# Streamed operands of a hybrid decoder trunk at the lower end of SBUF, weights and constants at the upper end

## The chip, the cores and the metric

The kernel runs on one core of one Trainium2 chip. The metric is the device time of one execution in microseconds (us). Beside timed runs there is one execution taken by the hardware profiler; it has a time of its own.

## What is computed

The reference is a trunk of two layers on a sequence of 1,024 positions with 1,024 features in float32. Cut to what matters:

```python
for layer in range(2):
    hn = rms_norm(h, norm_mix_g[layer])
    if layer % 2 == 0:   # gated DeltaNet heads and short convolutions
        h = h + mixer_ab(hn, ab_w_in[i], ..., ab_w_out[i])
    else:                # HGRN2 heads and dilated window attention
        h = h + mixer_cd(hn, cd_w_in[i], ..., cd_w_out[i])
    hn = rms_norm(h, norm_ffn_g[layer])
    h = h + (silu(hn @ ffn_w_gate[layer]) * (hn @ ffn_w_up[layer])) @ ffn_w_down[layer]
return rms_norm(h, norm_final_g)
```

The hidden size of the FFN is 2,816, or 22 blocks of 128. Nearly all the work is matrix products: the mixers' input and output projections, and the three products of each FFN.

## The kernel before, in words

Features lie on the 128 partitions, positions along the free dimension, in two halves of 512 positions. A float32 number is kept as a pair of fp32r numbers, high and low (`split`, lines 100 to 103: ScalarE makes the high part, VectorE or GpSimd the rest), and a product of two such pairs is three matmuls, written by `mm3` at lines 126, 127 and 128: high by high, high by low, low by high. Each streams 512 columns of an activation operand past a stationary 128 x 128 block of weights. `v_rows` (lines 989 to 999) is the exception: there the activations are stationary and the weights are streamed, 256 columns at a time.

The stages are, in order: mixer_ab (layer 0), its output projection, the FFN's gate and up stage (class Up), the FFN's down stage (`down`), and the same with mixer_cd for layer 1.

**Up** computes gate and up of a block f of 128 hidden units for both halves of the sequence with seven half-size products instead of eight, from sums and differences of operands and weights. Its streamed operands are b11, b21 (names hn in the profile), t1 and b22, and t2, t3 and t4. Per block f there are seven products (p1, p2, p5, p6, p7 and the two in `end`), each 4 x 3 = 12 matmuls. The first three blocks are ordered by hand (`turn`, under a manual schedule); the rest is ordered by the scheduler of the language, by priorities and its own estimate of times.

**down** multiplies hidden activations, read back from DRAM into the tile hr and split into a tile hidq, by the down weights. One hidq tile holds two blocks f (high, low, high, low). The line

```python
p, b = (hx, 6) if n[0] % 14 < 6 else (hnp, 8)
```

(512) puts the n-th hidq tile into the pool hx or into the pool hnp. Each of the 8 output blocks d streams all 22 blocks f.

**Memory.** A pool is a stretch of SBUF that grows from the left (low addresses) or the right (high addresses), in the order in which pools are opened; a closed pool's bytes are used again, and the new tile waits for the last use of the old ones on its bytes. Addresses are bytes within a partition. The low 16,512 bytes are taken by the run time, and usable memory ends at 229,344. Before the change the compiled program has these places:

| pool | what it holds | side | bytes |
|---|---|---|---|
| ring | weights: 4 split units `w` (8 KiB each), 2 raw buffers (4 KiB) | left | 16,512 to 57,472 |
| hnp | 8 slots of 8 KiB: hn, b11, b21, t1, b22, hidq | left | 57,472 to 123,008 |
| const | constants (cf, ci, vec, ones and so on) | left | 123,008 to 127,968 |
| sums (in Up) | a spare raw buffer and the sums of weights `ws` | left | 128,000 to 136,192 |
| hx (in Up) | 6 slots of 8 KiB: high and low parts of t2, t3, t4 | left | 136,192 to 185,344 |
| hx (in down) | 6 slots of 8 KiB: hidq | left | 127,968 to 177,120 |
| hr (in down) | 4 buffers of 2 KiB: hidden activations from DRAM | left | 177,120 to 185,312 |
| up (in Up) | 2 more weight units `w`, hid, u2, c22 | right | 196,480 to 229,248 |

The mixers' own pools lie behind const on the left and at the upper end on the right. Small tiles named "pad" (96 bytes in Trunk.begin, lines 163 and 164, and in Up.run, line 399; 32 bytes in Up.turn, line 403) shift what lies behind them.

All transfers are issued on SyncE's queue (`dma`, line 56), in the order that the scheduler gives them. The pools are opened at lines 66 to 70 and, for Up, at lines 1469 and 1470; `down` gets its pools at lines 1477 to 1479.

Of the kernel before, what the change touches and what calls it, by code (L numbers as in the profile page):

```python
# [9 lines left out]
F32 = mybir.dt.float32  # L10
# [8 lines left out]
P = 128  # L19
# [33 lines left out]
def hybrid_trunk_kernel(ctx: ExitStack, tc: tile.TileContext, x_t, w_all, w_down, w_ba, vecs, c_f, c_i, c_rope, out):  # L53
# [4 lines left out]
    def pool(name, side="left", space=None):  # L58
        kw = {} if space is None else {"space": space}
        if space is None:  # L60
            kw["side"] = side
        if space is not DRAM:
            kw["reuse_waits"] = "tile"
        return tc.tile_pool(name=name, bufs=1, **kw)

    ring = ctx.enter_context(pool("ring"))
    hnp = ctx.enter_context(pool("hnp"))
    const = ctx.enter_context(pool("const"))
    ps = ctx.enter_context(pool("ps", space=PSUM))
    dr = ctx.enter_context(pool("dr", space=DRAM))  # L70


    cf = const.tile([P, C_RM], F32, name="cf")
# [11 lines left out]
    onesn = const.tile([P, 1], F32, name="onesn")  # L85
    V.memset(onesn, 1.0 / DM)
    mhalf = const.tile([P, 16], F32, name="mhalf")
    V.memset(mhalf, -0.5)

    def psg():  # L90
        return ps.tile([P, HT], F32, tag="g", name="psg", bufs=2)
# [4 lines left out]
    def psm():  # L96
        return ps.tile([P, HT], F32, tag="m", name="psm", bufs=3)


    def split(hi, lo, src, eng=V):  # L100

        S.copy(hi, src)  # L102
        eng.tensor_tensor(lo, src, hi.bitcast(F32), op=SUB)  # L103

    def unit():

        return ring.tile([P, 2, DM], F32R, tag="w", name="w", bufs=4)

    def wload(*names):

        us = []
        for n in names:
            us.append(unit())
            raw = ring.tile([P, DM], F32, tag="raw", name="raw", bufs=2)
            dma(raw, w_all[W_AT[n]])
            split(us[-1][:, 0, :], us[-1][:, 1, :], raw)
        return us
# [21 lines left out]
    def quarter(pool_=None, name="hn"):  # L139

        p, n = (hnp, 8) if pool_ is None else (pool_, 6)
        return tuple(p.tile([P, KH, HT], F32R, tag="hn", name=name + "hl"[z], bufs=n) for z in range(2))
# [5 lines left out]
    class Trunk:  # L148
# [10 lines left out]
        def begin(self, half, src):  # L159

            self.h[half] = [self.hp.tile([P, KH, HT], F32, tag=f"h{half}{i}", name=f"h{half}{i}", bufs=1)
                            for i in range(2)]
            if half == 1:
                self.hp.tile([P, 24], F32, name="pad")
            for d in range(KT):
                dma(self.at(half, d), src[:, d, :])

# [78 lines left out]
    class Up:  # L246
# [133 lines left out]
        def run(self, tr, row, b11, b21, hx, close, left, right):  # L380

            E = mybir.EngineType
            with tc.manual_schedule(engines={E.PE, E.DVE, E.Activation, E.Pool}):
                b22, t3, t4 = self.turn(tr, row, b11, b21, hx, close, left, right)
            t1, t2 = self.t12
            self.weights(3)
            self.p7(2, t3)
            for f in range(3, NF):
                if f > 3:
                    self.weights(f)  # L390
                self.p1(f, b11)
                self.p2(f, b21, psm())
                self.end(f - 1, t4, b22)
                self.c11(f)
                self.p6(f, t2)
                self.p5(f, t1, psg())
                self.p7(f, t3)
            self.end(NF - 1, t4, b22)
            self.right.tile([P, 24], F32, name="pad")

        def turn(self, tr, row, b11, b21, hx, close, left, right):

            self.left.tile([P, 8], F32, name="pad")
            for f in range(2):
                self.part_a(f, self.raw("g", f))
            u0 = self.raw("u", 0, True)
            self.part_a(2, self.raw("g", 2))
            g0 = self.raw("g", 0)
            s = self.sums(g0, u0)
            G.tensor_tensor(u0[:, :HT], g0[:, :HT], u0[:, :HT], op=SUB)  # L410
            G.tensor_tensor(g0[:, HT:], g0[:, HT:], s[:, :HT], op=SUB)
            low = self.prepared(0, s, "s2", "s1")
            self.p1(0, b11)
            dg = tr.rms(1, between=low)
            self.p2(0, b21, psg())
            pb = tr.spread(dg)
            self.p1(1, b11)
            self.p2(1, b21, psg())
            self.p1(2, b11)
            self.p2(2, b21, psm())  # L420
            tr.short.close()
            self.snaps = left("snaps")

            (a0, b0), (a1, b1) = tr.h[0], tr.h[1]
            lo, hi = slice(0, 2), slice(2, 4)
            t1, b22 = quarter(name="t1"), quarter(name="b22")
            t2, t3, t4 = quarter(hx, "t2"), quarter(hx, "t3"), quarter(hx, "t4")
            self.t12 = t1, t2

            def comb(dst, x, y, c):  # L430
                V.tensor_tensor(dst[:, c, :], x[:, c, :], y[:, c, :], op=SUB)

            def high(t, src):
                for c in (lo, hi):
                    S.copy(t[0][:, c, :], src[:, c, :])

            def rest(t, src):
                for c in (lo, hi):
                    V.tensor_tensor(t[1][:, c, :], src[:, c, :], t[0][:, c, :].bitcast(F32), op=SUB)

            tr.scale(1, row, pb, (0,))
            self.part(0, u0, "s3", "a22")
            g1 = self.snap(0)
            u1 = self.raw("u", 1)
            tr.scale(1, row, pb, (1, 2, 3))
            comb(a0, a1, a0, lo)
            comb(a0, a1, a0, hi)
            high(t1, a0)
            s = self.left.tile([P, DM], F32, tag="s", name="ws", bufs=1)
            G.tensor_tensor(s[:, HT:], u1[:, :HT], u1[:, HT:], op=ADD)  # L450
            w1 = self.raw("g", 1, True)
            tr.scale(1, row, pb, range(KH, KT))
            rest(t1, a0)
            low_d = self.prepared(0, g0, None, "s4")
            self.p5(0, t1, psm())
            V.tensor_tensor(s[:, :HT], s[:, HT:], w1[:, :HT], op=SUB)
            low = self.prepared(1, s, "s2", "s1")
            comb(a0, b1, a0, lo)
            low()
            self.p5(1, t1, psm())  # L460
            comb(a0, b1, a0, hi)
            high(t2, a0)
            rest(t2, a0)
            g2 = self.snap(1)
            comb(a1, b1, a1, lo)
            comb(a1, b1, a1, hi)
            high(t3, a1)
            self.p6(0, t2)
            self.p6(1, t2)
            self.add11(0, g1)  # L470
            self.add11(1, g2)
            rest(t3, a1)
            V.tensor_tensor(u1[:, :HT], w1[:, :HT], u1[:, :HT], op=SUB)
            low = self.prepared(1, u1, "s3", "a22")
            comb(b0, b0, a0, lo)
            low()
            comb(b0, b0, a0, hi)
            high(t4, b0)
            low_d()
            u2 = self.raw("u", 2)  # L480
            rest(t4, b0)
            high(b22, b1)
            V.tensor_tensor(w1[:, HT:], w1[:, HT:], s[:, :HT], op=SUB)
            rest(b22, b1)
            close()
            self.right = right("up")
            self.part(1, w1, None, "s4")
            self.first = [self.hidden()]
            w2 = self.raw("g", 2)
            self.loads = 1  # L490
            s = self.sums(w2, u2)
            self.p7(0, t3)
            self.p7(1, t3)
            self.part_b(2, s)
            self.end(0, t4, b22)
            self.end(1, t4, b22)
            self.c11(2)
            self.p5(2, t1, psg())
            self.p6(2, t2)
            self.part_c(2, w2, u2)  # L500
            self.part_d(2, w2, s)
            return b22, t3, t4
# [920 lines left out]
    dma(cf[:, 0:P], c_f[:, 0:P])  # L1423
    dma(vec, vecs)
    first = [wload(("ab", 0), ("ab", 4)), wload(("ab", 8), ("ab", 12))]
    tr.begin(1, x_t[1])
    dma(cf[:, P:], c_f[:, P:C_RM])
    dma(ci, c_i)
# [15 lines left out]
    for layer in range(2):  # L1444
# [21 lines left out]


        with ExitStack() as fes:
            up = Up(layer, fes.enter_context(pool("sums")))
            hx = fes.enter_context(pool("hx"))  # L1470
            up.run(tr, row, *b1, hx, es.close, lambda n: fes.enter_context(pool(n)),
                   lambda n: fes.enter_context(pool(n, side="right")))

# [2 lines left out]
        with ExitStack() as fes:  # L1476
            hx = fes.enter_context(pool("hx"))
# [98 lines left out]
```

## Time and profile before

| | us |
|---|---|
| median of 3 runs | 2832.07 |
| lowest and highest run | 2829.3, 2838.61 |
| the profiled execution, its own time | 2837.84 |
| its span, first to last instruction | 2836.1 |

The mean granted clock of TensorE in the profiled execution is 0.987 of full speed.

How to read the rows: a line such as "L126 PE MATMUL psu<-t4h,w 128*128 128x512 f32" is one matmul of source line 126 that streams the tile t4h past weights w into the PSUM tile psu, 512 columns long. In the timeline the first column is the start in us from the span's start, the second the duration. Matmuls overlap, so the pace of TensorE is the difference of starts and not the duration. In the groups, "x176 | 69.3, 394 | 0.0" is the count, the busy us, the mean ns of one, and the idle us ahead of them with what ended it. PE is TensorE's matmuls, PEld its weight loads, DVE VectorE, ACT ScalarE, POOL GpSimd, SPq SyncE's queue of transfers.

### The profile page before, as it was taken

What the parts mean: (1) busy time and instruction counts of PE and PEld (TensorE: products, weight loads), DVE (VectorE), ACT (ScalarE), POOL (GpSimd) and SP (SyncE); (2) the same over time, 40 slices, a digit from 0 to 9 for tenths busy, and PEclk for the clock granted to TensorE, in tenths of its full rate; (3) what the DMA queues carried; (4) which work ended last, traced back from release to release, by engine and by line L of the source; (5) the groups of instructions that cost most, each with busy time, mean ns of one, the idle gap of its engine ahead of it and who ended that gap; (6) DMA issues with size and microseconds to landing.
All of it is one profiled execution on the core that took longest, in us unless ns stands there. A gap on an engine that the chain in (4) does not pass through costs nothing.

```text
span 2836.1 us, 37934 instructions
## 1 busy us (share of the span) xinstructions
PE 2730.9 (96%) x14974; PEld 2227.2 (79%) x14974; DVE 1502.4 (53%) x2599; ACT 1004.7 (35%) x1733; POOL 477.5 (17%) x435
## 2 busy tenths in 40 slices
PE   7999999989999989999999999999998999998998
PEld 5788877768787868889788897887876878876886
DVE  8766555573433343534765756666566334334342
ACT  5432122343333332323444434444434333333221
POOL 0110111333333201010000000000034333320000
PEclk9999999999999999999999999999999999999999
DMA  3334345522222274442132121323742222227442
GB/s 134 107 107 159 91 151 166 166 78 86 82 77 88 82 252 127 142 129 75 46 86 83 57 90 46 86 83 90 244 131 82 83 81 82 75 91 245 123 139 70
DMA packets 166178, 312.82 MB, mean 110 GB/s; under 512 B 22992, under 2 KB 70384, under 8 KB 164848
## 3 DMA queue, kind: packets, MB, share of 16 engines
q1 hardware_dynamic: 166000, 310.40, 34.8%
q8 instruction: 117, 1.92, 0.3%
q14 instruction: 61, 0.50, 0.1%
HBM read 236.32 MB, written 74.01 MB: 109 GB/s over the span
## 4 chain that ended last, share of the span: by engine, by line
PE 78%; DVE 8%; DMA 6%; ACT 4%; issue 3%; POOL 1%; SPq 0%; POOLq 0%; DVEq 0%; ACTq 0%
PE psu L126 17%; PE psu L128 16%; PE psu L127 16%; PE psm L128 4%; PE psm L127 4%; PE psm L126 4%; PE psg L128 3%; PE psg L127 3%; PE psg L126 3%; DMA hr<-hid 1%; DMA raw<-in_dram 1%; DVE w L103 1%; PE psm L1254 1%; DMA cxb<-scr_c 1%; DMA h<-hd 1%
## 5 line engine op out<-in xcount | busy, mean ns | idle before, releaser
L103 DVE TENSOR_TENSOR w<-raw,w 128x1024 fp32r<-128x1024 f32 (+1 forms) x336 | 408.6, 1218 | 610.2 <-ACT w L102 607.7
L102 ACT CAST w<-raw 128x1024 fp32r<-128x1024 f32 (+1 forms) x336 | 327.4, 975 | 649.6 <-PE psm L128 313.4
L126 PE MATMUL psu<-hnh,w 128*128 128x512 f32 x1328 | 532.0, 402 | 3.4 <-ACT w L102 1.9
L127 PE MATMUL psu<-hnl,w 128*128 128x512 f32 x1328 | 526.9, 397 | 0.5 <-DVE hnl L103 0.5
L128 PE MATMUL psu<-hnh,w 128*128 128x512 f32 x1328 | 524.8, 395 | 0.5 <-DVE w L103 0.5
L126 PEld LDWEIGHTS psu<-hnh,w 128*128 128x128 f32 x1328 | 250.7, 189 | 56.7 <-ACT hnh L102 3.5
L128 PEld LDWEIGHTS psu<-hnh,w 128*128 128x128 f32 x1328 | 250.9, 189 | 52.8 <-DVE w L103 1.6
L127 PEld LDWEIGHTS psu<-hnl,w 128*128 128x128 f32 x1328 | 250.7, 189 | 51.9 <-DVE hnl L103 1.9
L182 POOL TENSOR_TENSOR acc<-acc,sq 128x512 f32<-128x512 f32 x48 | 75.5, 1573 | 517.0 <-ACT sq L181 449.8
L126 PE MATMUL psm<-hidq,w 128*128 128x512 f32 x352 | 141.3, 401 | 19.0 <-ACT hidq L102 18.9
L126 PE MATMUL psu<-w,hnh 128*128 128x256 f32 x512 | 149.9, 293 | 0.0
L127 PE MATMUL psu<-w,hnh 128*128 128x256 f32 x512 | 145.3, 284 | 0.0
L128 PE MATMUL psu<-w,hnl 128*128 128x256 f32 x512 | 145.2, 284 | 0.0
L127 PE MATMUL psm<-hidq,w 128*128 128x512 f32 x352 | 141.5, 402 | 2.9 <-DVE hidq L103 2.9
L128 PE MATMUL psm<-hidq,w 128*128 128x512 f32 x352 | 140.1, 398 | 0.0
L126 PE MATMUL psu<-hidq,w 128*128 128x512 f32 x352 | 139.1, 395 | 0.0
L128 PE MATMUL psu<-hidq,w 128*128 128x512 f32 x352 | 138.6, 394 | 0.0
L127 PE MATMUL psu<-hidq,w 128*128 128x512 f32 x352 | 138.3, 393 | 0.0
L295 POOL TENSOR_TENSOR raw<-raw,ws 128x512 f32<-128x512 f32 x40 | 55.8, 1395 | 327.5 <-DVE w L103 327.5
L126 PEld LDWEIGHTS psu<-w,hnh 128*128 128x128 f32 x512 | 98.4, 192 | 0.8 <-issue 0.2
L127 PEld LDWEIGHTS psu<-w,hnh 128*128 128x128 f32 x512 | 98.4, 192 | 0.3 <-issue 0.2
L128 PEld LDWEIGHTS psu<-w,hnl 128*128 128x128 f32 x512 | 98.3, 192 | 0.0
(384 smaller groups left out, 5416.5 us busy)
## 6 DMA issues: line engine op xcount, KB each, us to landing
raw<-in_dram SPq DMA_DIRECT2D x270, 512.0 KB, 3.6
hid<-hid SPq DMA_DIRECT2D x88, 256.0 KB, 2.0
hr<-hid SPq DMA_DIRECT2D x88, 256.0 KB, 3.6
hd<-h SPq DMA_DIRECT2D x48, 256.0 KB, 3.4
raw<-in_dram SPq DMA_DIRECT2D x32, 384.0 KB, 3.1
h<-hd SPq DMA_DIRECT2D x48, 256.0 KB, 6.0
scr_c<-cx SPq DMA_DIRECT2D x8, 1216.0 KB, 4.6
cxb<-scr_c SPq DMA_DIRECT2D x8, 1216.0 KB, 6.0
```

The costliest lines, as they stand in the source:

```text
L102: S.copy(hi, src)
L103: eng.tensor_tensor(lo, src, hi.bitcast(F32), op=SUB)
L126: T.matmul(o, lh, rh, start=first and i == 0, stop=False, **kw)
L127: T.matmul(o, lh, rl, start=False, stop=False, **kw)
L128: T.matmul(o, ll, rh, start=False, stop=last and i == n - 1, **kw)
L182: (eng or (V if d == KT - 1 else G)).tensor_tensor(a, a, q, op=ADD)
L295: G.tensor_tensor(a[:, HT:], a[:, HT:], s[:, :HT], op=SUB)
L1254: T.matmul(o[:, 0:n * P], q[:, j * P:(j + 1) * P], k[:, (j - n + 1) * P:(j + 1) * P], start=True, stop=True)
```

## The change

The pools ring and const go to the right side, so they lie at the upper end of SBUF; hnp is the first pool of the left side. For Up, hx is opened ahead of sums, so that it lies right behind hnp. Three pads go and two new ones come: 32 bytes in const, 96 bytes in ring. No instruction is added, removed or altered but for its addresses, and tile counts and sizes stay.

```diff
@@ hybrid_trunk_kernel
-    ring = ctx.enter_context(pool("ring"))
     hnp = ctx.enter_context(pool("hnp"))
-    const = ctx.enter_context(pool("const"))
+    ring = ctx.enter_context(pool("ring", side="right"))
+    const = ctx.enter_context(pool("const", side="right"))
     ps = ctx.enter_context(pool("ps", space=PSUM))
     dr = ctx.enter_context(pool("dr", space=DRAM))
...
     mhalf = const.tile([P, 16], F32, name="mhalf")
+    const.tile([P, 8], F32, name="pad")
     V.memset(mhalf, -0.5)
@@ Trunk.begin
-            if half == 1:
-                self.hp.tile([P, 24], F32, name="pad")
@@ Up.run
             self.end(NF - 1, t4, b22)
-            self.right.tile([P, 24], F32, name="pad")
@@ Up.turn
-            self.left.tile([P, 8], F32, name="pad")
@@ hybrid_trunk_kernel
     first = [wload(("ab", 0), ("ab", 4)), wload(("ab", 8), ("ab", 12))]
+    ring.tile([P, 24], F32, name="pad")
     tr.begin(1, x_t[1])
...
         with ExitStack() as fes:
+            hx = fes.enter_context(pool("hx"))
             up = Up(layer, fes.enter_context(pool("sums")))
-            hx = fes.enter_context(pool("hx"))
             up.run(tr, row, *b1, hx, es.close, lambda n: fes.enter_context(pool(n)),
                    lambda n: fes.enter_context(pool(n, side="right")))
```

## The prediction

> **What bounds the kernel now.** I read the page first: busy shares, granted clock.
>
> ```profile
> PE 2730.9 (96%) x14974; PEld 2227.2 (79%) x14974; DVE 1502.4 (53%) x2599; ACT 1004.7 (35%) x1733; POOL 477.5 (17%) x435
> PEclk9999999999999999999999999999999999999999
> ```
>
> TensorE is busy nearly all the time at nearly full clock, and no other engine comes near it. An average can hide stages with another limit, so I then read the windows: busy time of each engine in stretches of 100 us.
>
> ```profile
> 700.00:800.00 100.00, 100.00 (x432) 80.05 (x431) 38.31 (x41) 33.69 (x47) 38.06 (x28) 1.00 0.27 86
> 1000.00:1100.00 100.00, 89.05 (x366) 68.52 (x365) 40.66 (x50) 34.04 (x49) 8.24 (x5) 0.95 0.66 214
> 1200.00:1300.00 100.00, 100.00 (x486) 83.43 (x485) 47.91 (x66) 31.40 (x44) 8.94 (x7) 1.00 0.33 107
> 1300.00:1400.00 100.00, 98.66 (x825) 85.27 (x825) 58.61 (x112) 39.88 (x77) 3.33 (x6) 1.00 0.24 71
> ```
>
> The columns are PE, PEld, DVE, ACT, POOL, clock, DMA share, GB/s. The first row is the FFN's gate and up stage of layer 0, the second the beginning of its down stage, the last two the end of it and the projections of layer 1. Only the beginning of the down stage (and the chunk recurrence of layer 0, not shown) leaves TensorE visibly idle. In all the rest the time is a count of matmuls times the distance between the starts of two of them. Busy time can't show that distance, because matmuls are pipelined: one lasts 0.39 us, yet 432 start in 100 us, one every 231 ns. So I went to the timeline of TensorE and took differences of starts. This is the view that decides here.
>
> Gate and up stage, inside one hidden block f:
>
> ```profile
> 806.77 0.40 PE L126 MATMUL psu<-t4h,w 128*128 128x512 f32 x1
> ...
> 809.56 0.39 PE L126 MATMUL psg<-b22h,w 128*128 128x512 f32 x1
> ...
> 810.26 0.39 PE L126 MATMUL psg<-b22h,w 128*128 128x512 f32 x1
> ...
> 814.34 0.39 PE L126 MATMUL psg<-t1h,w 128*128 128x512 f32 x1
> ...
> 814.98 0.39 PE L127 MATMUL psu<-t2l,w 128*128 128x512 f32 x1
> ...
> 817.54 0.39 PE L127 MATMUL psg<-t1l,w 128*128 128x512 f32 x1
> ```
>
> Twelve steps with t4 as the streamed operand take 809.56 - 806.77 = 2.79 us, 232.5 ns each. Eleven with t2 take 2.56 us, 232.7 ns. Eighteen with b22 and t1 take 4.08 us, 226.7 ns. Same shape, same type, same weights' ring, same engine, no wait between them. What differs is the pool of the streamed operand: b22 and t1 lie in hnp (57,472 to 123,008 bytes), t2 to t4 in hx (from 136,192).
>
> The down stage is the better test, since there one loop fills both pools with the same kind of tile (hidq), by the same lines:
>
> ```profile
> 1216.93 0.39 PE L127 MATMUL psm<-hidq,w 128*128 128x512 f32 x1
> ...
> 1221.46 0.40 PE L126 MATMUL psu<-hidq,w 128*128 128x512 f32 x1
> ...
> 1229.88 0.40 PE L126 MATMUL psu<-hidq,w 128*128 128x512 f32 x1
> ```
>
> The first two rows enclose 20 steps on hnp slots, 4.53 us, 226.5 ns each. The last two enclose the 36 steps of f = 4 to 15 of the second half, whose six slots are those of hx (127,968 to 177,120): 8.42 us, 233.9 ns each. So **where the streamed operand lies costs 5.9 ns per matmul in the gate and up stage (232.6 against 226.7) and 7.4 ns in the down stage.** The border lies between 123,008 and 127,968.
>
> **The change part by part.** No instruction is added or taken away; only addresses move. hnp goes to 16,512 to 82,048, hx right behind it to 82,048 to 131,200, the ring to 188,288 and up, the constants to 183,296. What each move is worth:
>
> *hx into the fast stretch.* How many matmuls stream from it comes from the counts of the groups:
>
> ```profile
> L127 PE MATMUL psu<-t4l,w 128*128 128x512 f32 x176 | 69.3, 394 | 0.0
> L126 PE MATMUL psm<-hidq,w 128*128 128x512 f32 x352 | 141.3, 401 | 19.0 <-ACT hidq L102 18.9
> L128 PE MATMUL psu<-w,hnl 128*128 128x256 f32 x512 | 145.2, 284 | 0.0
> ```
>
> t2, t3 and t4 have nine groups of 176 (three operands by three lines), 1,584. hidq has six of 352, 2,112; the slot counter `n[0] % 14 < 6` puts 5 of 11 pairs of the first half and 6 of 11 of the second into hx, so 1,056. The gain is 1,584 x 5.9 ns = 9.3 us and 1,056 x 7.4 ns = 7.8 us, together 17.1 us. All of it is on the path: nothing but TensorE is near its limit in those stages.
>
> *The tail behind a slow product.* After the t3 product the stream goes back to hnp, but not at once to its speed:
>
> ```profile
> 801.73 0.40 PE L128 MATMUL psu<-hnh,w 128*128 128x512 f32 x1
> ...
> 804.05 0.39 PE L126 MATMUL psm<-hnh,w 128*128 128x512 f32 x1
> ```
>
> Ten steps on hnp in 2.32 us, 232.0 ns, 53 ns more than ten at 226.7. With 44 blocks f in two layers that is 2.3 us, and I take it to go too: 19.4 us.
>
> *The last slot of hx.* It covers 123,008 to 131,200. Before, an operand from 127,968 on was slow, and nothing was streamed between 123,008 and there. The slot holds t2l (176 matmuls) and a sixth of the down stage's 1,056. If it stays slow, 176 x 5.9 + 176 x 7.4 = 2.3 us are lost; I take half, 1.2.
>
> *The ring into the slow stretch.* Weights are mostly the stationary operand, but v_rows streams them (the 3 x 512 matmuls of 256 columns in the last row above). They run fast now:
>
> ```profile
> 1299.83 0.28 PE L127 MATMUL psu<-w,hnh 128*128 128x256 f32 x1
> ...
> 1301.99 0.28 PE L127 MATMUL psu<-w,hnh 128*128 128x256 f32 x1
> ```
>
> 18 steps in 2.16 us, 120.0 ns. At the top they cost nothing if the shorter stream hides it, 1,536 x 7.4 = 11.4 us if the price is one per matmul, and half, 5.7 us, if it goes with the columns. I take 5.7, since half the row is streamed. As the stationary operand, weights cost nothing at the top. In one block of three the products of t1 take weights from the pool "up" at 223,104, the upper end:
>
> ```profile
> 792.80 0.39 PE L126 MATMUL psg<-t1h,w 128*128 128x512 f32 x1
> ...
> 794.84 0.39 PE L126 MATMUL psg<-t1h,w 128*128 128x512 f32 x1
> ```
>
> Nine steps in 2.04 us, 226.7 ns, as with ring weights at 32,896.
>
> *All other tiles.* The splits of VectorE cost the same into both pools:
>
> ```profile
> L439 DVE TENSOR_TENSOR t2l<-h,t2h 128x1024 fp32r<-128x1024 f32 x4 | 4.8, 1222 | 0.0
> L439 DVE TENSOR_TENSOR b22l<-h,b22h 128x1024 fp32r<-128x1024 f32 x4 | 4.7, 1217 | 0.0
> ```
>
> Nothing there, and VectorE has half its time free to cover a few ns.
>
> *Which tile sits on whose bytes.* A new tile waits for the old readers of its bytes. In the down stage hr lay on t2l, which the product p6 of the last block reads; now it lies on "sums", free since the last weights were split. The first load went out at 996.53, that split at 974.91. The stage's waits and the 16 loads of h that stand in SP's queue between operands:
>
> ```profile
> 996.53 0.37 SPq L516 DMA_DIRECT2D hr<-hid  x1
> ...
> 1008.33 11.02 SPq L166 DMA_DIRECT2D h<-hd  x16
> ```
>
> ```profile
> PE psm L126 <- ACT hidq L102: 18.9, 5, 9.5
> ```
>
> ```profile
> 974.91 0.69 DVE L103 TENSOR_TENSOR w<-raw,w 128x512 fp32r<-128x512 f32 x1 [3.45 <-ACT w L102]
> ```
>
> Earlier operands could save half of the 18.9 us at best; a queue order with the block of h one place earlier could cost some 5. The order is made by the scheduler, which I don't follow here: value 0, ends -9.4 and +5. No wait is added anywhere else, and the pads cost no instruction.
>
> **Sum:** -19.4 + 1.2 + 5.7 = -12.5 us. The profiled execution took 2837.84 us (span 2836.1 and 1.7 around it) and would come to 2825.3. It was 5.8 us above the median of the runs, 2832.07; against that the forecast is **2819.6 us**.
>
> The Trainium skill speaks against this change. Its page "SBUF — State Buffer", section "Who interferes with whom", says that PE never waits on anyone and knows contention only as a lock on a port, and its page "TensorE: Matmul & The Clock Gate", section "Back-to-back issue gap", gives the distance of two matmuls as columns over 2.4 GHz plus 2.5 ns, 215.8 ns for 512 columns, with no term for the address. By these pages of the Trainium skill the sum is 0. The trace disagrees with both: its best runs stand at 226.5 and its hx runs at 233.9.
>
> **The rivals.**
> 1. *The ring pays in full and the last slot stays slow:* -19.4 + 11.4 + 2.3 = -5.7 us, 2826.4. For it: in 256 columns there is less time to hide a fixed price. Against: nothing shows the price to be fixed.
> 2. *The address is not the cause.* hx and hnp differ in something that travels along: in the down stage hx began 96 bytes off a multiple of 128, and in both stages its neighbours (hr, snaps, sums) are written while it is read. Then hx stays slow in its new place, 2832. Against: t2 to t4 lay on a multiple of 128 and were slow as well, and the ring, the busiest neighbour of all, touches hnp without harm. The two pages of the Trainium skill named above would give the same time.
> 3. *Slower: the fast stretch is the middle, not the low end.* No stream of 512 columns came from below 57,472 before. hnp's lower five of eight slots move to 16,512 to 57,472. The groups of 512 columns, of which this is one of the three largest,
>
> ```profile
> L126 PE MATMUL psu<-hnh,w 128*128 128x512 f32 x1328 | 532.0, 402 | 3.4 <-ACT w L102 1.9 <-ACT hnh L102 1.5
> ```
>
> add up to 9,648 matmuls of the helper mm3, less the 2,640 of hx 7,008; five eighths are 4,380, at about 6.2 ns 27 us. The tails stay, v_rows loses nothing (its ring was then slow already): -17.1 + 1.2 + 27 = +11, 2843. It decides from 16/4,380 = 3.7 ns per matmul on. Against: the ring lay in just that stretch and its streams of 256 columns took 120.0 ns; 226.7 - 120.0 = 106.7 ns for 256 further columns leaves both lengths the same 13.3 ns of overhead, so the ring was as fast as hnp.
> 4. *The beginning of the down stage moves* by the ends above: about 2812 when earlier, 2837 when later.
>
> **How the numbers follow.** Forecast 0.52; rival 1 0.14; rival 2 0.11; rival 3 0.13; rival 4 0.07 earlier, 0.03 later. A measurement of this kernel can tell 0.3%, 8.5 us, from no change: faster means below 2823.6, slower above 2840.6. Faster 0.52 + 0.07 = 0.59; same 0.14 + 0.11 + 0.03 = 0.28; slower 0.13. The range leaves out rival 3 and the later half of rival 4: from -19.4 with 6 us saved at the down stage, 2806, to rival 2 and the spread of the runs, 2834.
>
> **What would show it.** Right: differences of starts of 227 ns for t2 to t4 and for all hidq rows; more than 432 matmuls per 100 us in the gate and up stage (some 437); v_rows at 122 to 127 ns. Wrong: t2 to t4 still at 232 ns (rival 2); b22, t1 or hn rows above 230 ns away from any tail (rival 3); v_rows at 127 ns or more (rival 1); a wait for hidq longer than 9.5 us (rival 4). Any change of VectorE's or ScalarE's durations would break the step that leaves them out.

## The result and the profile after

The changed kernel takes 2815.57 us (median of 4 runs, 2808.89 to 2818.09), the kernel before 2831.28 beside it (4 runs): ratio 0.9936, 95% interval 0.9911 to 0.9961. The profiled execution after took 2816.07 us (span 2814.3), 21.8 less than the profiled one before. By the medians it is 15.7 less; the same kernel before, run again beside the later kernels, had medians of 2834.05 to 2836.09. Either is more than the 12.5 of the prediction's sum, and it lies elsewhere. The stages of the two profiled executions, cut at the starts of the first t1 matmul and of the first and last hidq matmul of each layer, in us:

| stage | before | after | difference |
|---|---|---|---|
| gate and up, layer 0 and 1 | 427.5, 428.2 | 426.3, 427.4 | -1.2, -0.7 |
| down, layer 0 and 1 | 261.5, 261.7 | 251.6, 251.8 | -9.9, -9.9 |
| all the rest | 1457.3 | 1457.2 | -0.1 |

The gate and up stage was to give 11.6 us and gave 1.9. The down stage was to give 7.8 and gave 19.8. v_rows was to lose 5.7 and lost nothing.

First the page after, and three windows:

```profile
PE 2717.7 (97%) x14974; PEld 2228.3 (79%) x14974; DVE 1499.3 (53%) x2599; ACT 1004.1 (36%) x1733; POOL 475.5 (17%) x435
```

```profile
700.00:800.00 100.00, 100.00 (x433) 80.29 (x432) 37.93 (x41) 33.70 (x47) 37.67 (x28) 1.00 0.26 87
1000.00:1100.00 100.00, 92.90 (x396) 74.89 (x395) 40.98 (x52) 33.75 (x47) 8.22 (x5) 0.97 0.64 212
1100.00:1200.00 100.00, 100.00 (x445) 82.54 (x444) 48.59 (x58) 36.51 (x50) 8.79 (x6) 1.00 0.47 146
```

The last of them before:

```profile
1100.00:1200.00 100.00, 100.00 (x437) 81.14 (x436) 47.14 (x56) 35.92 (x49) 7.07 (x5) 1.00 0.44 135
```

The gate and up stage still starts 433 matmuls in 100 us (before 432). The down stage starts 445 (before 437), and at its beginning 396 where there were 366. Now the timeline of TensorE, down stage, 36 steps on the six slots of hx:

```profile
1197.24 0.39 PE L128 MATMUL psm<-hidq,w 128*128 128x512 f32 x1
...
1205.40 0.39 PE L128 MATMUL psm<-hidq,w 128*128 128x512 f32 x1
```

8.16 us, 226.7 ns each (before 233.9), its last slot included. In the gate and up stage t4, with weights from the ring, has gained as forecast:

```profile
807.08 0.39 PE L128 MATMUL psu<-t4h,w 128*128 128x512 f32 x1
...
809.80 0.39 PE L128 MATMUL psg<-b22h,w 128*128 128x512 f32 x1
```

Twelve steps in 2.72 us, 226.7 ns. But one block later t3, in the same pool:

```profile
818.89 0.39 PE L129 MATMUL psu<-t3l,w 128*128 128x512 f32 x1
...
821.46 0.40 PE L130 MATMUL psu<-hnh,w 128*128 128x512 f32 x1
```

Eleven steps in 2.57 us, 233.6 ns. Its weights lie in the pool "up", at 150,528. The pool's two units were at 196,480 and 221,056 before, and t1's products on them ran at 226.7. v_rows, with the ring at the top:

```profile
1299.05 0.28 PE L129 MATMUL psu<-w,hnh 128*128 128x256 f32 x1
...
1302.41 0.28 PE L130 MATMUL psu<-w,hnl 128*128 128x256 f32 x1
```

28 steps in 3.36 us, 120.0 ns, as before. Last the transfers of hr at the beginning of the down stage of layer 0 (the tile's own view, 970 to 1025 us), before and then after, and the wait for hidq after:

```profile
L516 SPq DMA_DIRECT2D hr<-hid x12: 319/370/888, 996.5 to 1021.8; - x12
```

```profile
L514 SPq DMA_DIRECT2D hr<-hid x15: 319/320/1162, 972.3 to 1021.8; - x15
```

```profile
PE psm L128 <- ACT hidq L104: 13.2, 4, 5.9
```

The first loads of hr go out 24 us earlier. Their bytes were those of sums, whose last reader, a split of ws, ended at 970.7; before, they were those of t2l, and the last t2 matmul started at 992.2. The wait for hidq falls from 18.9 to 13.2 us. Over both layers the differences of starts split the down stages' 19.8 us into 8.5 of pace (mean of all steps of 200 to 260 ns: 231.0 before, 227.0 after, 1,056 steps a layer) and 11.3 of shorter waits, which is what remains.

### The profile page after: what moved, and what is told of

The parts are those of the page before. It is cut to its first block, busy times and chain, and to the rows that moved or that the text cites. A ratio compares the mean times of both kernels' runs of the same rounds, so it can differ in the third digit from the quotient of the medians.

```text
span 2814.3 us, 37936 instructions
## 1 busy us (share of the span) xinstructions
PE 2717.7 (97%) x14974; PEld 2228.3 (79%) x14974; DVE 1499.3 (53%) x2599; ACT 1004.1 (36%) x1733; POOL 475.5 (17%) x435
## 4 chain that ended last, share of the span: by engine, by line
PE 80%; DVE 8%; DMA 5%; ACT 4%; issue 2%; POOL 1%; SPq 0%; POOLq 0%; DVEq 0%; ACTq 0%
PE psu L128 17%; PE psu L130 17%; PE psu L129 17%; PE psm L128 4%; PE psm L130 4%; PE psm L129 4%; PE psg L130 3%; PE psg L128 3%; PE psg L129 3%; DVE w L105 1%; PE psm L1252 1%; DMA hr<-hid 1%; PE psm L1270 1%; DMA h<-hd 1%; DMA cxb<-scr_c 1%
## 5 line engine op out<-in xcount | busy, mean ns | idle before, releaser
L128 PE MATMUL psm<-hidq,w 128*128 128x512 f32 x352 | 139.8, 397 | 13.2 <-ACT hidq L104 13.2
```

Of the source, the lines that this page charges most:

```text
L128: T.matmul(o, lh, rh, start=first and i == 0, stop=False, **kw)
```

## The experiments

After these traces the theory was: **the address**. A stretch from about 128 KiB to 185,000 bytes is slow for TensorE, for the streamed operand and for the stationary weights alike; the fast place is not "the low end" but anything outside it. Rivals: **neighbours** (other engines write in that stretch), and the prediction's own picture. The waits of the down stage were held to be a matter of their own.

**A map of the addresses.** The kernel is replaced by runs of matmuls on an otherwise idle core (cut to what matters):

```python
def run(w, m, n):
    for i in range(n):
        c = slice(i % 4 * P, i % 4 * P + P)
        T.matmul(p, a[w][:, c], a[m], start=i == 0, stop=i == n - 1)
for i in range(101): run(0, i, 36)
for i in range(101): run(i, 1, 36)
```

> Leaves out the whole computation: SBUF is filled with 101 fp32r tiles of 2 KiB from 18,560 to 225,408, and then only TensorE works, in runs of 36 matmuls of 128x512, first with the streamed operand stepped through all tiles (weights at 18,560), then with the weights stepped through all tiles (operand at 20,608), then in pairs. Address theory: the pace of a run rises by 4 to 8 ns per matmul when the streamed operand lies between about 128 KiB and some border in 183,000 to 188,288, and by as much when the weights lie there; no step anywhere else, the lowest and the highest tiles at one pace. Neighbours theory (traffic of other engines in the same stretch): no step, one pace within 1 ns, as nothing else works. Theory of the prediction (low end fast, everything above 128 KiB slow for streams, weights free): a step up at 128 KiB for streams that never goes back, none for weights.

Two windows, the first with the streamed operand at 57,000 to 83,000, the second at 163,000 to 188,000, inside the supposed stretch:

```profile
200.00:300.00 100.00, 100.00 (x442) 82.81 (x442) 0.00 (x0) 0.00 (x0) 0.00 (x0) 1.00 0.00 0
...
620.00:720.00 100.00, 100.00 (x442) 82.83 (x442) 0.00 (x0) 0.00 (x0) 0.00 (x0) 1.00 0.00 1
```

Each of the 202 runs stands at 226.6 or 226.7 ns. The address theory has fallen, and with it the prediction's: these tiles show no slow stretch.

**The two halves of the change.** "swap" is the kernel before with only

```diff
+            hx = fes.enter_context(pool("hx"))
             up = Up(layer, fes.enter_context(pool("sums")))
-            hx = fes.enter_context(pool("hx"))
```

> The kernel before with one part of the change alone: hx is opened ahead of sums. hx stays in the slow stretch (127,968 to 177,120), hr of the down stage lies on the bytes of sums, not of t2l. If half of the down stages' gain is the earlier loads of hr: the wait for hidq at the helper's first line falls from 18.9 to about 13 us, the down stages shorten by 4.5 to 6 us each, the pace of hidq matmuls stays at 231 ns, total -9 to -12 us (2820 to 2823). If all of it is pace: within 2 us of before, wait still 19.

and "sides" is the changed kernel with those lines as before.

> The change without the swap: ring and constants at the upper end, but sums ahead of hx as before (sums 82,048 to 90,240, hx 90,240 to 139,392 in the gate and up stage, 82,048 to 131,200 in the down stage, hr on the bytes of t2l). If address and waits add up: the down stages keep the pace of 227 ns (-4.2 us each) but the wait for hidq stays at 18 to 19 us; total -9 to -11 us. If the swap is what makes the fast pace (neighbours next to hx): pace of hidq at 231, total within 3 us of before. If the ring at the top makes the shorter wait: wait 13, total -20.

swap: 2827.24 us, ratio 0.9973 (0.9961 to 0.9985). sides: 2826.89, 0.9968 (0.9955 to 0.9981). One window and the wait of each, swap first:

```profile
1100.00:1200.00 100.00, 100.00 (x437) 81.20 (x437) 47.75 (x58) 36.91 (x51) 7.06 (x5) 1.00 0.46 142
```

```profile
PE psm L126 <- ACT hidq L102: 12.8, 3, 6.1
```

```profile
1100.00:1200.00 100.00, 100.00 (x445) 82.57 (x444) 47.87 (x57) 36.73 (x50) 7.06 (x5) 1.00 0.45 140
```

```profile
PE psm L128 <- ACT hidq L104: 16.8, 4, 8.6
```

swap has the old pace and the short wait, sides the new pace and nearly the old wait. The down stages shorten by 5.1 and 6.2 us in swap and by 5.0 and 5.7 in sides, together 22.0 where the change gives 19.8. So the two gains are separate, and the wait belongs to the place of hr. Both totals gain some 7 us where 9 to 12 were expected. swap loses 2.5 to 3.0 us in each gate and up stage, which was not expected: the mean step of t2 to t4 between 640 and 970 us rises from 232.8 to 234.5 ns, though they moved by only 8 KiB. No later run explains this rise. sides, like the change, gains nothing to speak of in the gate and up stage.

**Without the units of "up".**

```diff
-            u = self.right.tile([P, 2, DM], F32R, tag=f"w{i % 6}", name="w", bufs=1) if i >= 0 and i % 6 < 2 else unit()
+            u = unit()
```

> The change, and the gate and up stage splits all its weights into the ring at 188,288 and up; the two more units of the pool up (150,528 and 175,104) go, so six units become four. Address theory, for weights as well as streams: the pace of that stage goes from 229.8 to 227 ns, 1,848 matmuls per layer, -5 us per layer, total -10 us against after (2805), less what the shorter lookahead brings in waits for weights. If only streams count: pace stays at 229.8, total 2815 or above. If four units are too few: waits for w show behind split, over 5 us per layer.

2808.45 us, ratio 0.9905 (0.9885 to 0.9926), about 7 below after where 10 were expected. The two intervals overlap, but the stages show it: gate and up take 6.9 and 6.0 us less than in after. The window of the gate and up stage:

```profile
700.00:800.00 100.00, 100.00 (x440) 82.03 (x439) 39.26 (x41) 34.20 (x47) 42.03 (x28) 1.00 0.25 82
```

440 matmuls against 433. The weights' place counts as well as the operand's, and four units are enough. But why a place counts was open again, since the map denied it.

**A second map, with what the first lacked:** random numbers, high and low parts, the helper's order of three, and at the end other engines at work.

> Leaves out the whole computation. Again TensorE is timed at 23 addresses from 22,656 to 205 thousand, but with what the first map lacked: first with all ones, then with random numbers in high and low parts (x of the input, split as the kernel splits), in runs of one tile and in the helper's pattern high by high, high by low, low by high; at the end the same pattern while VectorE and ScalarE copy within about 60, 150 and 200 thousand. Theory that the numbers' bits matter: ones at 226.7 everywhere, random numbers 5 to 8 ns slower where operand or weights lie in 131,072 to about 185,000. Theory that the pattern of three matters: only the runs in threes are slower there. Theory of neighbours' traffic: only the last part is slower, and only where the copies go to the stretch that is streamed. None of the three: 226.7 throughout, and what makes the kernel's stretch slow is still not in the test.

None of the three. A window in which VectorE and ScalarE copy next to the streamed tiles:

```profile
1260.00:1360.00 100.00, 100.00 (x443) 82.80 (x442) 72.81 (x248) 92.85 (x229) 0.00 (x0) 1.00 0.00 1
```

226.7 ns throughout. That agrees with the Trainium skill, page "SBUF — State Buffer", section "Who interferes with whom", which says that PE never waits on anyone. The neighbours theory has fallen too, as far as VectorE and ScalarE go; GpSimd and transfers were not in the test.

So I looked for what every fast pair of the kernels has in common and no slow one, and found the **start addresses modulo 256**, the rest that an address leaves on division by 256 (in brackets):

| tile | before | after |
|---|---|---|
| hnp (hn, t1, b22, hidq) | 57,472 (128) | 16,512 (128) |
| units of the ring | 16,512 (128) | 188,288 (128) |
| hx, gate and up | 136,192 (0) | 82,048 (128) |
| hx, down | 127,968 (224) | 82,048 (128) |
| units of "up" | 196,480, 221,056 (128) | 150,528, 175,104 (0) |

All tiles of both maps began at 128 modulo 256, which is why they saw nothing. By this table 2,640 of mm3's 9,648 matmuls with 512 columns had operand and weights at different starts before (the 1,584 of t2 to t4 by 128 bytes, 1,056 of hidq by 96). After, the 1,152 with weights in "up" have (48 products a layer, by 128).

**A third map, of the offsets.**

```python
for a in range(16):
    for b in range(16):
        run(w0[:, 8 * a:], m0[:, 8 * b:], 30)   # 8 elements are 32 bytes
```

> Leaves out the whole computation. TensorE alone, random numbers, runs of 30 matmuls in which the streamed operand begins 0 to 480 bytes (steps of 32) behind a tile at 16,512 (128 modulo 256) and the weights 0 to 480 bytes behind one at 20,608 (128 modulo 256), all 256 pairs; a few at 141,440 as well, in steps of 4 bytes, and with 256 columns. Theory of the offset modulo 256: 226.7 ns only where the start is 128 modulo 256, some 6 to 8 ns more at 0 modulo 256 and in between, for the streamed operand and for the weights; same at 141,440. Should only the difference of the two starts count, pairs on one diagonal are fast. Address or neighbours theory: 226.7 in all pairs, as in the first two maps, whose tiles all began at 128 modulo 256.

Three windows, one run of 30 matmuls each (the counts include those that overlap the window's ends): weights 0 and operand 0 bytes behind; operand 32 behind; and weights and operand both 32 behind:

```profile
23.00:29.80 6.80, 6.80 (x32) 5.63 (x30) 0.00 (x0) 0.00 (x0) 0.00 (x0) 1.00 0.02 2
29.80:36.80 7.00, 7.00 (x32) 5.63 (x30) 0.00 (x0) 0.00 (x0) 0.00 (x0) 1.00 0.00 0
...
141.42:148.25 6.83, 6.83 (x32) 5.63 (x31) 0.00 (x0) 0.00 (x0) 0.00 (x0) 1.00 0.01 2
```

The same 30 matmuls take 6.80, 7.00 and 6.83 us. From the starts, ns per matmul by the operand's start minus the weights', modulo 256 (weights at offset 0, mean of the last 17 steps of each run):

| bytes | 0 | 32 | 64 | 96 | 128 | 160 | 192 | 224 |
|---|---|---|---|---|---|---|---|---|
| 512 columns | 226.6 | 233.2 | 228.7 | 233.5 | 233.6 | 234.5 | 233.4 | 233.2 |
| 256 columns | 120.0 | 117.8 | 117.8 | 120.2 | 118.9 | 117.5 | 113.4 | 118.5 |

Only the **difference** counts: all 32 pairs on the diagonals of difference 0 stand at 226.6 or 226.7, whichever start the two share. At 141,440 it is the same. With 256 columns the best difference is another one, 192. The first steps of a run show one thing more: a run with equal starts that follows a slow one begins slowly (mean of all its steps 226.9 to 227.6), and one that follows another with equal starts doesn't (226.7).

**The offset alone, before and after.** "padhx" is the kernel before, moved nowhere, with hx at 128 modulo 256; "afteroff" the changed kernel with hx at 0:

```diff
             hx = fes.enter_context(pool("hx"))
+            hx.tile([P, 32], F32, name="pad")
...
             hx = fes.enter_context(pool("hx"))
+            hx.tile([P, 40], F32, name="pad")
```

These are the two places of padhx, gate and up stage and down stage; afteroff has 32 in both.

> The kernel before, nothing moved to another end of memory, but a pad of 128 bytes at the beginning of hx in the gate and up stage and of 160 bytes in the down stage, so that hx begins at 128 modulo 256 (before: 0 and 224). Offset theory: the pace of hidq goes from 231.0 to 227 ns, that of the gate and up stage from 230.8 to 227.2, the wait for hidq stays at 18 to 19 us; total 4.2 per down stage and 6 to 7 per gate and up stage, -20 to -23 us (2812). Theory of the prediction (low end against upper end): nothing changes, 2832 to 2834.

> The change, but hx begins with a pad of 128 bytes in both stages, so that it lies at the low end (82,176 to 131,328) at 0 modulo 256. Offset theory: the pace of hidq rises from 227 to 230 to 231 ns, that of the gate and up stage to 232 or more, total +12 to +16 us against after (2828 to 2832). Theory of the prediction: as after, 2815 to 2817.

padhx: 2822.85 us, ratio 0.9957 (0.9941 to 0.9973). afteroff: 2821.89, 0.9958 (0.9944 to 0.9972). The down stage of padhx, then of afteroff:

```profile
1100.00:1200.00 100.00, 100.00 (x444) 82.61 (x443) 48.77 (x58) 37.35 (x51) 7.57 (x6) 1.00 0.46 145
```

```profile
1100.00:1200.00 100.00, 100.00 (x438) 81.36 (x438) 47.94 (x57) 36.48 (x50) 8.78 (x6) 1.00 0.47 146
```

With 160 bytes of padding hx is fast in its old place (444, before 437), and with 128 bytes it is slow at the low end (438, after 445). That settles it for the down stage: the offset is the cause, the end of memory is none. afteroff rises by 6 us over after and not by 12 to 16. Its four stages rise by 9.6, the rest of its profiled execution is 3.7 shorter. The gate and up stages give only 2.3 and 1.4 of it (230.4 ns a step where 232 or more was expected), as hx then shares the start 0 with the units of "up", and those pairs become fast; the down stages give 2.3 and 3.5.

padhx gave 11.7 us where 20 to 23 were expected. Its down stages gave 5.7 and 5.9, more than the 4.2 expected; its gate and up stages gave 3.2 and 2.2 instead of 6 to 7. The same shows in "padup", the changed kernel with a pad at the end of Up.run:

```diff
             self.end(NF - 1, t4, b22)
+            self.right.tile([P, 32], F32, name="pad")
```

> The change with a pad of 128 bytes at the end of the pool up, so that its two weight units begin at 150,400 and 174,976, 128 modulo 256 (in after 150,528 and 175,104, 0 modulo 256). They stay in the middle of memory. Offset theory: the pace of the gate and up stage goes from 229.8 to 227.2 ns, as with the units left out, total -8 to -10 us against after (2805 to 2808). Theory that the stretch 131,072 to 185,000 is slow: as after, 2815 to 2817.

2812.05 us, ratio 0.9923 (0.9908 to 0.9938), 3.5 below after instead of 8 to 10. The intervals of the two overlap, but the gate and up stages of the profiled executions are 1.8 and 1.3 us shorter. In padup the mean step of t4, b22, t1 and hn between 640 and 970 us is 226.7, on "up" as on the ring; but t2 stays at 230.6 and t3 at 231.0. Both products begin with a wait of the weight load on ScalarE, and some nine steps after it are slow (240, 230, 232, 236, 224, 231, 236, 228 and 233 ns in one case). The waits of the weight loads in that window, before, padup and ringonly:

```profile
PEld psu L126 <- ACT gt L326: 5.0, 16, 0.3
PEld psu L126 <- ACT u L348: 3.1, 17, 0.2
```

```profile
PEld psu L128 <- ACT gt L326: 5.3, 17, 0.3
PEld psu L128 <- ACT u L348: 3.3, 17, 0.2
```

```profile
PEld psu L128 <- ACT gt L326: 1.8, 6, 0.3
PEld psu L128 <- ACT u L348: 1.2, 6, 0.2
```

Two short waits in nearly each of 17 blocks, in before as in padup, and 6 of each in ringonly. What I had expected of padhx and padup was ringonly's pace, and part of ringonly's gain was that it has a third of these waits. Why it has fewer wasn't tried.

**Both side effects without the move.** Last, swap with a pad of 160 bytes at the beginning of hx in both stages:

> The kernel before with two small edits and nothing moved to another end: hx is opened ahead of sums, and a pad of 160 bytes puts hx at 128,128 (128 modulo 256) in both stages. If the change's gain is the sum of two side effects (start of the streamed operand against start of the weights modulo 256, and hr of the down stage on the bytes of sums), this has both, and the gate and up stage's units at the same offset besides: pace of hidq 227 ns, wait for hidq 11 to 14 us, total 2810 to 2816, no slower than the change. If the two ends of memory matter in themselves, it stays at least 6 us behind the change's 2815.6.

2814.10 us, ratio 0.9923 (0.9908 to 0.9938): the interval overlaps that of the change. Its down stages take 251.8 and 251.1 us, as short as the change's. No gain that these runs could tell is left for the two ends of memory.

**A better version.** "vshift" is ringonly with the weights of v_rows 192 bytes further in their units (the part of the edit that moves them):

```diff
-    def unit():
-        return ring.tile([P, 2, DM], F32R, tag="w", name="w", bufs=4)
+    def unit(off=0):
+        t = ring.tile([P, 2 * DM + 64], F32R, tag="w", name="w", bufs=4)
+        return t[:, off:off + 2 * DM].rearrange("p (z c) -> p z c", z=2)
...
-            us.append(unit())
+            us.append(unit(48 if n[0] == "cd" and n[1] // 2 * 2 in VPAIRS else 0))
```

> As the kernel with four ring units only, and the weights that are streamed 256 columns at a time begin 192 bytes later in their units, so that they start 192 bytes modulo 256 behind the stationary activations (before 0). For room, each ring unit is 256 bytes longer, two pools of the trunk keep one tile sq in place of two, a tile tq takes the buffer of another named t, and const lies outermost. By the map with 256 columns (113.4 ns at 192 bytes, 120.0 at 0): the pace of v_rows goes from 120 to 113.4 ns, 1,536 x 6.6 = -10 us against the kernel with four ring units (2808), 2798. Should 512 and 256 columns follow one rule (equal offsets are best), the pace goes up. If tq or sq delay VectorE and ScalarE on the path, part of the 10 us is lost.

2799.58 us, ratio 0.9876 (0.9857 to 0.9894), the fastest here. The timeline in v_rows:

```profile
1305.67 0.28 PE L129 MATMUL psu<-w,hnh 128*128 128x256 f32 x1
...
1310.90 0.28 PE L130 MATMUL psu<-w,hnl 128*128 128x256 f32 x1
```

46 steps in 5.23 us, 113.7 ns, as the map had it. Other stretches of v_rows stand at 117.8. Over all its steps up to 140 ns the mean falls from 119.7 in ringonly to 115.6, which is 6.3 us for 1,536 matmuls and not 10. The medians differ by 8.9, in runs of different sittings whose intervals overlap, so the rest of that is not shown to be v_rows'. Why some stretches stay at 117.8 wasn't tried.

## Why the prediction came out near, and what was wrong in it

The time and the direction came out right, but the cause was not the one named, and the terms were wrong: the gate and up stage gave 9.7 us less than forecast, v_rows 5.7 and the beginning of the down stage 11.3 more. These errors have opposite signs and cancel in part; that the forecast, 2819.6, came within 4 us of the median is luck.

1. **"Where the streamed operand lies costs 5.9 ns per matmul in the gate and up stage ... and 7.4 ns in the down stage": the rows were right, the reading of them wrong.** Every slow row compared there had its operand at another start modulo 256 than its weights, or followed such rows. I weighed alignment in rival 2 and dropped it because "t2 to t4 lay on a multiple of 128 and were slow as well". 128 was the wrong modulus, and the partner was missing: an operand is not aligned by itself, but against the weights. The move repaired hx because its new place happens to start at 128 modulo 256.
2. **The gate and up term, -11.6 expected, -1.9 measured.** The step that failed is "As the stationary operand, weights cost nothing at the top". It looked at the units of "up" where they lay and did not ask where they would land: 1,152 matmuls went from equal starts to a difference of 128. padup, which only repairs this, gains 3.1 us in the two stages. The other part: t2 and t3 were priced at the full 5.9 ns, but keep slow steps after their waits. Comparing padup with before they gain 1.5 and 2.6 ns, and t4 5.9. The steps after a slow product, priced at 2.3 us, did turn fast where the pairs are in step: hn goes from 229.2 to 226.7 ns.
3. **The down stage's pace, -7.8 expected, -8.5 measured**, the last slot with it. The 1.2 us set aside for that slot weren't needed.
4. **v_rows, +5.7 expected, 0 measured.** There was no slow stretch to move into; weights and activations kept equal starts, and 120.0 ns.
5. **The beginning of the down stage, 0 expected, -11.3 measured.** I had named the mechanism (hr on sums instead of t2l) and its two times, and took the middle of -9.4 and +5 because of the order in SP's queue. swap shows it alone, and after, padup, afteroff and padswap, which have that order of hx and sums, wait 11.3 to 13.2 us for hidq against 16.4 to 18.9 in before, sides and padhx (14.2 in ringonly and 16.7 in vshift, which have it too; why they wait longer wasn't followed). The prediction took a split of weights at 974.91 for the last reader of sums; the loads went out before it, from 972.3 on. The lower end was too near as well: "half of the 18.9" counted only the wait that the profile names, and that wait fell by only 5.7; the rest of the 11.3 lies in other gaps of the stage.
6. **"Nothing there" for VectorE's splits** held: 1502.4 us busy before, 1499.3 after.

So: -8.5 - 1.9 + 0 - 11.3 = -21.7, where the prediction had -19.4 + 1.2 + 5.7 = -12.5. Rival 3 (fast middle) is refuted by the first map, where tiles from 18,560 up all stand at 226.6 or 226.7. The formula that the prediction cites for 215.8 ns is, in the Trainium skill, page "TensorE: Matmul & The Clock Gate", section "Back-to-back issue gap", that of an isolated matmul. The fastest steps of 512 columns here stand at 226.6 ns. What stays open is why 256 bytes and why a difference matters at all, and why a wait or a slow product is followed by some nine slow steps.

## What to carry to other kernels

Before you explain a matmul's pace by where a tile lies, write down the starts of both operands modulo 256 and compare each pair: a pad of some bytes in a pool can be worth as much as a new layout, and any pool that is moved takes its own tiles out of step with their partners. Price a move for everything that it displaces, also for tiles that the change doesn't name. When a map of one variable is flat, look for what all its points have in common.

## What the runs showed of the hardware

- On an otherwise idle core (map and map3), an fp32r matmul of 512 columns starts every 226.6 to 226.7 ns when operand and weights start at equal addresses modulo 256, and every 228.7 to 234.5 ns when they differ by another multiple of 32 bytes. The address itself was worth nothing from 18,560 to 225,408.
- In steps of 4 bytes up to 124 (map3) the operand is fast again at differences of 28, 60 and 108 bytes (226.6 to 226.7) and slowest at 100 (240.0).
- With 256 columns (map3) the best difference among multiples of 32 bytes is 192: 113.4 ns, half of 226.7; equal starts take 120.0.
- The Trainium skill, page "SBUF — State Buffer", section "Who interferes with whom", gives PE two independent read ports, one for the streamed operand and one for the weights. The pace by their difference, 226.6 against 233.2, is not that of two reads that know nothing of each other; which part of the chip joins them no run here shows.
